# A hybrid decoder layer: X and Y products of the first two feed-forward blocks issued ahead of the column sums, T1 product third, activations loaded into their operand tiles

## The chip, the cores and the metric

The kernel runs on one core of one Trainium2 chip. The metric is the device time of one execution in microseconds (us); lower is better. The kernel before took 2458.94 us, the median of three runs (2458.13 to 2459.27).

## The reference

One inference step of one decoder layer in float32, for a prompt of 2048 tokens and for 8 decode tokens that each extend a cache of their own. The model width is 1024, the feed-forward width 2816. Cut to what matters:

```python
z = rms_norm(x, norm_mix_g) @ w_in              # q, k, v and the conv branch
...                                             # banded attention; GLU, conv of width 31, LayerNorm, silu
h = x + jnp.concatenate([attn_o, conv_o], axis=-1) @ w_out
fg, fu = jnp.split(rms_norm(h, norm_ffn_g) @ w_ffn_in, 2, axis=-1)
ffn_ext = jnp.concatenate([ffn_hist.astype(fg.dtype), fg], axis=1)
fc = causal_dwconv(ffn_ext, ffn_conv_w, ffn_conv_b)           # width 3
h = h + (jax.nn.gelu(fc, approximate=False) * fu) @ w_ffn_out
gate = jax.nn.sigmoid(rms_norm(h, norm_ple_g) @ w_ple_gate)
h = h + (p @ w_ple_proj) * gate
```

## The kernel before, in words

**Halves.** Tokens lie along the free dimension. The prompt is worked in two halves of 1024 tokens; half 1 also holds the 8 decode tokens. For each half come, in this order, the output projection (`w_out_unit`), the feed-forward up-projection with its gate (`ffn_in`, 22 blocks f of 128 gate rows and 128 up rows), and the down-projection (`ffn_out`). Half 0 does all three, then half 1. Last comes the gate with the per-layer embedding, in eight units m.

**Products.** TensorE (PE) multiplies float32 numbers as a high and a low part: `hilo` (L211) copies a tile into its high part on ScalarE (ACT, L212) and subtracts to get the low part on VectorE (DVE, L213), and every product takes three matmuls, hi·hi, hi·lo, lo·hi (L195, L196, L197).

**Seven products for eight.** `ffn_in` doesn't multiply the normed activations B by the weights directly. The activations of a half are cut in four blocks: features 0–511 and 512–1023 by tokens 0–511 and the rest, named B11, B21, B12, B22. The weights of an f are cut in four too, and seven block products of sums take the place of eight (a Strassen-Winograd scheme). Its operands are B11, B21, B22 and the sums T1 = B12 − B11, T2 = B22 − T1, T3 = B22 − B12 and T4 = B21 − T2. Every operand is split into high and low. On the weight side an f has four tiles: hg (the two blocks a11, a12), hs and ht (sums of blocks), and w (a22).

**The order of the products in an f.** X = hg·B11 (copied by ACT, L1152), Y = hg·B21 (summed by DVE into the gate rows, L1155), T2 added to X (copied, L1157), Z = ht·T1 (copied, L1160), T3 added to X (copied, L1162), B22 added to Z (summed by DVE, L1164), T4 added to X. X is one accumulator in PSUM; each copy has to be made before the next product may add to it. In half 0 a block is 512 columns wide, so an f has 84 matmuls of 512; in half 1 there are two blocks, of 256 and 264 columns (GROUPS), so 168 narrower ones. Then `gate` (L1131) makes gelu of the width-3 convolution: ACT L1133, DVE L1135 and L1136, for the decode tokens L1139 and L1140, and the gelu on ACT, L1141. DVE multiplies by the up rows (L1169) and the result is stored to DRAM (actd, L1170). The same is done for the second token block (L1172 to L1174).

**Weights.** Class W (L79 to L166) loads raw tiles of 512 KB (two buffers) through SyncE's queue (SP, L106), builds the sums on DVE (L138 to L141, all in place in the raw tiles but L138's s1f) and splits them into `whl` tiles (three buffers) and w (one buffer). For an f two raw tiles come: one with a11 and a12 (g), one with a21 and a22 (u). L138 adds a21 and a22; the raw tile of u is free when the low part of w is made.

**Building the operands.** `build_T` (L1070) waits for the row norms of the second token block: `stats` (L721) sums the columns of squares with matmuls by ones (L725), DVE copies the sums (L732), POOL takes the root, `bcast` (L735) transposes the result back to all partitions (rb, L738, L739), and a chain of some fifty DVE instructions (L1098 to L1117, with `hilo`'s) forms T2, T1, T3, B22 and T4. B11 and B21 are ready before, from the output projection's last part (`w_out_second`, `hn_k`).

**The down-projection.** `ffn_out` (L1182) loads the activations of a block from DRAM into a staging tile `as` (three buffers, L1193) and splits them with `hilo` into a tile `act`, which takes the place of an operand tile that is no longer needed.

**Beside it.** The width-31 convolution of half 1 runs on DVE (L403, L406) in pieces: `bg(ns)` issues as many of its steps as ns nanoseconds hold, after each f of the up-projection (5500) and each weight tile of the down-projection (3000).

**What sets the order.** A scheduler decides in which order the instructions stand on each engine, from the order of the code and from priorities. Each engine then works through its list in order; an instruction that waits holds back all behind it on its engine.

Of the kernel before, what the change touches and what calls it, by code (L numbers as in the profile page):

```python
# [7 lines left out]
F32 = mybir.dt.float32  # L8
# [9 lines left out]
KD = 8  # L18
# [15 lines left out]
def hybrid_layer_kernel(ctx: ExitStack, tc: tile.TileContext, I, O):  # L34
# [176 lines left out]
    def hilo(hi, lo, src):  # L211
        AC.copy(hi, src)  # L212
        DV.tensor_tensor(lo, src, hi.bitcast(F32), op=ALU.subtract)  # L213

    def rstd(dst, ss, tmp, cols, n):
# [529 lines left out]

    def hn_k(R, half, k, gi, rb, o, n):

        t = h_stage(half, k, o, n)
        lo = o % 512
        DV.scalar_tensor_tensor(t, t, gains[:, gi, k:k + 1], rb[:, o:o + n], op0=ALU.mult, op1=ALU.mult)  # L750
        hilo(R[k][:, 0, lo:lo + n], R[k][:, 1, lo:lo + n], t)
# [295 lines left out]
    def w_out_second(half, R, acc, rt, Rb, step, xs=None, xpool=None):  # L1047

        rb = st_tile("rb")
        for m in range(KD):  # L1050
            w_out_unit(half, R, m, C1[half], acc, xs, xpool)
            step()
            if m == 0:
                stats(acc, rt, 0, 512)
            if m == 1:
                bcast(rt, rb, 0, 512)
            for k in spread(m, 2):
                hn_k(Rb, half, k, 1, rb, 0, 512)
# [10 lines left out]

    def build_T(half, Rb, rb, acc, rt, w2, w1, wt, w3, wb, w4_):  # L1070
# [5 lines left out]
        t1 = [conv_p.tile([128, RW], F32, tag="co", bufs=5, name="t1f")[:, :n] for _ in range(4)]  # L1076
# [20 lines left out]
        for k in range(4):
            DV.scalar_tensor_tensor(b22[k], b22[k], gains[:, 1, k + 4:k + 5], bc, op0=ALU.mult, op1=ALU.mult)  # L1098
# [19 lines left out]
        return Rb[:4], Rb[4:], T2, T1, T3, B22, T4  # L1118

    def ffn_in(half, RT, f):  # L1120
        B11, B21, T2, T1, T3, B22, T4 = RT
        hg, (hs, ht), h22 = W.get(0), W.get(1), W.get(2)
        ext, sa, sb = st_tile("ext"), st_tile("snA"), st_tile("snB")
        if half == 0:
# [20 lines left out]
        last = GROUPS[half][-1][0]  # L1145
        for o, n in GROUPS[half]:
            n0 = min(n, 512 - o)
            s1, s2 = sa[:, o:o + n], sa[:, RW + o:RW + o + n]
            s5, s3 = sb[:, o:o + n], sb[:, RW + o:RW + o + n]
            X = mtile("X")  # L1150
# [11 lines left out]
            AC.copy(s3, X[:, :n])  # L1162
# [8 lines left out]
            GP.tensor_tensor(s3, s3, s5, op=ALU.add)  # L1171
        t = gate(512, tot)  # L1172
        DV.tensor_tensor(t[:, :tot], t[:, :tot], sb[:, RW:RW + tot], op=ALU.mult)
        SY.dma_start(actd[f][:, 512:512 + tot], t[:, :tot])  # L1174
        if half == 0:
            GP.tensor_copy(fhist[:, f, :], ext[:, HALF:HALF + 2])
        else:
            GP.tensor_copy(fnew[:, f, :], ext[:, HALF:HALF + 10])
        W.done(3)
        bg(5500)  # L1180

    def ffn_out(half, acc, where, step=None, done=None):  # L1182
# [4 lines left out]
        def prep(n):  # L1187
            while len(acts) < min(n, NF * len(pcs)):
                p, f = divmod(len(acts), NF)
                o, c = pcs[p]  # L1190
                a, = new_R("act", [where[len(acts)]])
                t = s2_tile("as")
                SY.dma_start(t[:, :c], actd[f][:, o:o + c])  # L1193
# [29 lines left out]


    RT = build_T(0, Rb, rb, acc, rts[0], [2] * 4, [2] * 4, [2] * 4, [1] * 4, [1] * 4, [2] * 4)
    step_ns[0] = 2500
    bg_list += [conv_piece(conv_p, 2), conv_piece(conv_p, 3), conv_dec(conv_p, st_p)]
    for f in range(NF):
        ffn_in(0, RT, f)
    acc2 = acc_tile("acc2")  # L1230
# [35 lines left out]
    Rb = new_R("bB", [1] * 4 + [2] * 4)  # L1266
    rb = w_out_second(1, Rm1, accB, rts[2], Rb, lambda: None, xs, co_tile)
    RT = build_T(1, Rb, rb, accB, rts[2], [2] * 4, [1] * 4, [1] * 4, [2] * 4, [1] * 4, [1] * 4)
    for f in range(NF):
        ffn_in(1, RT, f)  # L1270
    acc3 = acc_tile("acc3")
# [198 lines left out]
```

## Time and profile before

| | |
|---|---|
| Time, median of 3 runs | 2458.94 us (2458.13 to 2459.27) |
| The profiled execution's own time | 2448.64 us |
| Its span | 2446.8 us |
| Mean granted clock of TensorE | 0.985 |
| TensorE (PE) busy | 2343.6 us, 96% |
| VectorE (DVE) busy | 1743.2 us, 71% |
| ScalarE (ACT) busy | 1190.9 us, 49% |
| GpSimd (POOL) busy | 289.7 us, 12% |

The profile is of one execution. A row of its timeline has the start, the duration, the engine, the line of the kernel, the operation, and the output and inputs by the program's names with their shape; in brackets stands how long the engine was idle before it and what ended that. SPq is SyncE's queue of transfers. A row of the waits names an engine's line, what it waited for, and then the microseconds in total, the number of times and the longest. A row of the windows has a stretch of the span, its length, the busy time of PE, of PE's weight loads (PEld), DVE, ACT and POOL with their counts, PE's clock, the busy share of the transfer engines and GB/s.

### The profile page before, as it was taken

The page shows a single profiled execution, that of the slowest core. Times are in us where ns is not written, and L with a number is a line of the kernel's source. Part 1 is how long each engine was busy: PE and PEld are TensorE (multiplying, and loading weights), DVE is VectorE, ACT ScalarE, POOL GpSimd, SP SyncE. Part 2 cuts the span into 40 slices and gives each one's busy share as a digit, 9 for nine tenths or more (in the row PEclk, how much of TensorE's full clock was granted, in tenths as well). Part 3 has the DMA queues.
Part 4 walks back from the last instruction along what each step waited for, and adds up shares of the span by engine and source line. Part 5 has one row for each costly group of instructions (what it writes and reads, how often), then busy time and mean ns, then how long its engine had stood idle before and what let it go on. Part 6 is the DMA issues. An engine that isn't in the chain of part 4 may idle for free.

```text
span 2446.8 us, 36723 instructions
## 1 busy us (share of the span) xinstructions
PE 2343.6 (96%) x13691; PEld 2035.5 (83%) x13691; DVE 1743.2 (71%) x2943; ACT 1190.9 (49%) x2183; POOL 289.7 (12%) x354
## 2 busy tenths in 40 slices
PE   7899999999799999999999999999999899999999
PEld 6777778877587777878878888999999899988888
DVE  4999899766899999997634478666666554565553
ACT  4566676755444445444523445444444443444443
POOL 3312122100012111220001101111111000000000
PEclk9999999999899999999999999999999999999999
DMA  8543422367232222246745741222222565776664
GB/s 293 171 127 119 157 77 86 115 202 239 72 98 90 82 82 86 91 132 204 240 134 186 222 150 57 78 79 79 79 79 79 162 222 191 216 222 192 200 187 114
DMA packets 357076, 348.19 MB, mean 142 GB/s; under 512 B 24414, under 2 KB 277784, under 8 KB 352770
## 3 DMA queue, kind: packets, MB, share of 16 engines
q1 hardware_dynamic: 336610, 333.25, 43.4%
q10 hardware_dynamic: 20288, 12.60, 1.8%
q8 instruction: 107, 1.75, 0.3%
q14 instruction: 71, 0.58, 0.1%
HBM read 271.61 MB, written 75.78 MB: 142 GB/s over the span
## 4 chain that ended last, share of the span: by engine, by line
PE 62%; DVE 19%; DMA 10%; ACT 4%; issue 3%; POOL 1%; SPq 0%; ACTq 0%; DVEq 0%; POOLq 0%
DVE co L406 6%; PE fo L196 5%; PE fo L197 5%; PE fo L195 5%; PE X L195 4%; PE X L196 4%; PE X L197 4%; DVE whl L213 3%; DMA raw<-in_w_ffn_in 2%; PE pg L197 2%; PE pg L195 2%; PE pg L196 2%; PE wo L195 2%; PE wo L197 2%; PE wo L196 2%
## 5 line engine op out<-in xcount | busy, mean ns | idle before, releaser
L213 DVE TENSOR_TENSOR whl<-raw,whl 128x1024 fp32r<-128x1024 f32 (+1 forms) x314 | 360.2, 1147 | 242.4 <-ACT whl L212 241.6
L212 ACT CAST whl<-raw 128x1024 fp32r<-128x1024 f32 (+1 forms) x314 | 310.3, 988 | 274.5 <-PE fo L197 113.7
L406 DVE SCALAR_TENSOR_TENSOR co<-gi,cvec,co 128x512 f32<-128x512 f32 x480 | 372.0, 795 | 3.1
L195 PE MATMUL fo<-act,whl 128*128 128x512 f32 (+2 forms) x880 | 308.6, 352 | 11.3 <-ACT act L212 9.8
L196 PE MATMUL fo<-act,whl 128*128 128x512 f32 (+2 forms) x880 | 310.3, 353 | 0.1
L197 PE MATMUL fo<-act,whl 128*128 128x512 f32 (+2 forms) x880 | 309.4, 352 | 0.9 <-DVE whl L213 0.9
L195 PE MATMUL X<-T,whl 128*128 128x512 f32 (+2 forms) x528 | 172.2, 327 | 19.6 <-ACT T L212 11.8
L195 PEld LDWEIGHTS fo<-act,whl 128*128 128x128 f32 x880 | 166.1, 189 | 28.1 <-ACT act L212 10.7
L197 PEld LDWEIGHTS fo<-act,whl 128*128 128x128 f32 x880 | 166.4, 189 | 17.1 <-DVE whl L213 1.3
L196 PEld LDWEIGHTS fo<-act,whl 128*128 128x128 f32 x880 | 166.7, 189 | 16.3 <-DVE act L213 1.0
L196 PE MATMUL X<-T,whl 128*128 128x512 f32 (+2 forms) x528 | 171.7, 325 | 1.5 <-DVE T L213 1.5
L197 PE MATMUL X<-T,whl 128*128 128x512 f32 (+2 forms) x528 | 170.3, 323 | 0.0
L1171 POOL TENSOR_TENSOR snB<-snB 128x256 f32<-128x256 f32 (+1 forms) x66 | 89.9, 1363 | 542.4 <-ACT snB L1162 542.4
L1141 ACT ACTIVATE ft<-ft 128x512 f32<-128x512 f32 (+2 forms) x110 | 60.3, 548 | 162.5 <-DVE ft L1136 119.5
L195 PEld LDWEIGHTS X<-T,whl 128*128 128x128 f32 x528 | 100.5, 191 | 33.6 <-ACT T L212 14.5
L195 PE MATMUL ag<-r,whl 128*128 128x512 f32 (+2 forms) x320 | 115.8, 363 | 0.0
L196 PE MATMUL ag<-r,whl 128*128 128x512 f32 (+2 forms) x320 | 114.3, 358 | 0.0
L197 PE MATMUL ag<-r,whl 128*128 128x512 f32 (+2 forms) x320 | 113.2, 354 | 0.0
L196 PEld LDWEIGHTS X<-T,whl 128*128 128x128 f32 x528 | 100.4, 190 | 10.6 <-DVE T L213 3.2
L197 PEld LDWEIGHTS X<-T,whl 128*128 128x128 f32 x528 | 100.8, 191 | 8.3 <-DVE whl L213 0.4
L1133 ACT ACTIVATE ft<-ext,fvec 128x512 f32<-128x512 f32 (+2 forms) x110 | 80.1, 728 | 49.0 <-DVE ext L1164 24.8
L212 ACT CAST act<-as 128x512 fp32r<-128x512 f32 (+2 forms) x110 | 57.5, 537 | 77.6 <-DMA as<-actd 76.1
(376 smaller groups left out, 6399.9 us busy)
## 6 DMA issues: line engine op xcount, KB each, us to landing
raw<-in_w_ffn_out SPq DMA_DIRECT2D x110, 512.0 KB
raw<-in_w_ffn_in SPq DMA_DIRECT2D x88, 512.0 KB
whl<-agd SPq DMA_DIRECT2D x24, 1024.0 KB
hs<-h SPq DMA_DIRECT2D x80, 256.0 KB
raw<-in_w_out SPq DMA_DIRECT2D x32, 512.0 KB
raw<-in_w_ple_gate SPq DMA_DIRECT2D x32, 512.0 KB
actd<-ft SPq DMA_DIRECT2D x44, 256.0 KB
as<-actd SPq DMA_DIRECT2D x44, 256.0 KB
```

What stands on the lines that cost most here:

```text
L195: PE.matmul(ps, wh, xh, start=first, stop=False, skip_group_check=more)
L196: PE.matmul(ps, wh, xl, start=False, stop=False, skip_group_check=more)
L197: PE.matmul(ps, wl, xh, start=False, stop=last, skip_group_check=more)
L212: AC.copy(hi, src)
L213: DV.tensor_tensor(lo, src, hi.bitcast(F32), op=ALU.subtract)
L406: DV.scalar_tensor_tensor(co[c], t[:, i:i + QT], cvec[:, c, i:i + 1], co[c], op0=ALU.mult, op1=ALU.add)
L1133: AC.activation(t[:, :n], ext[:, 2 + o:2 + o + n], func=AF.Identity, scale=w2, bias=bi)
L1141: AC.activation(t[:, :n], t[:, :n], func=AF.Gelu)
L1171: GP.tensor_tensor(s3, s3, s5, op=ALU.add)
```

## The change

It does these things:

- `ffn_in` is cut in three functions. `first` does X and Y of a block, `second` the other five products and the gate of the first token block, `finish` the second gate. `ffn_in_all` issues `first` of f = 0 and f = 1 for all blocks ahead of `build_T` (and so ahead of the column sums), then `second` and `finish` of both, and from f = 2 on all three in turn.
- In `second` T1 comes third, before T2; the order is X, Y, T1, T2, T3, B22, T4.
- `build_T` makes T1 first, then T2. `w_out_second` keeps the unsplit B11 in four tiles (b11), so that T1 is one subtraction, where the kernel before subtracted the high part and then the low part (L1100, L1101).
- `ffn_out` loads the activations straight into the low half of the tile `act`; `hl_inplace` makes the high part and then the low part in place. The staging tile is gone.
- `bg` after an f goes from 5500 to 4300 in half 0 and to 0 in half 1, in the down-projection from 3000 to 3700.
- In the last stage the column sums of the third norm are taken after unit m = 3 and not after m = 0. The residual rows of the output projection in half 1 come from another pool, and a memset goes ahead.

```diff
+    def hl_inplace(t, n):
+
+        v = t[:, 1, :n].bitcast(F32)
+        hilo(t[:, 0, :n], t[:, 1, :n], v)
...
         for k in range(4):
+            DV.scalar_tensor_tensor(b12[k], b12[k], gains[:, 1, k:k + 1], bc, op0=ALU.mult, op1=ALU.mult)
+            tt(t1[k], b12[k], t1[k], op=ALU.subtract)
+            split(T1[k], t1[k])
+        for k in range(4):
             DV.scalar_tensor_tensor(b22[k], b22[k], gains[:, 1, k + 4:k + 5], bc, op0=ALU.mult, op1=ALU.mult)
-            DV.scalar_tensor_tensor(b12[k], b12[k], gains[:, 1, k:k + 1], bc, op0=ALU.mult, op1=ALU.mult)
-            tt(t1[k], b12[k], f32(Rb[k], 0), op=ALU.subtract)
-            tt(t1[k], t1[k], f32(Rb[k], 1), op=ALU.subtract)
             tt(t2[k], b22[k], t1[k], op=ALU.subtract)
             split(T2[k], t2[k])
-        for k in range(4):
-            split(T1[k], t1[k])
...
-            mm_prod(X[:, :n], hs, 0, T2, o, n, False)
-            AC.copy(s2, X[:, :n])
+            return X
+
+        def second(o, n, X, RT):
...
             Z = mtile("Z")
             mm_prod(Z[:, :n], ht, 512, T1, o, n, True)
             AC.copy(s5, Z[:, :n])
+            mm_prod(X[:, :n], hs, 0, T2, o, n, False)
+            AC.copy(s2, X[:, :n])
             mm_prod(X[:, :n], ht, 0, T3, o, n, False)
...
+    def ffn_in_all(half, Rb, build, ns, start=None):
+        gs = GROUPS[half]
+        u0 = ffn_in(half, Rb, 0)
+        x0 = [u0.first(*g) for g in gs]
+        W.topup(4)
+        u1 = ffn_in(half, Rb, 1, 3)
+        x1 = [u1.first(*g) for g in gs]
+        RT = build()
...
-                t = s2_tile("as")
-                SY.dma_start(t[:, :c], actd[f][:, o:o + c])
-                hilo(a[:, 0, :c], a[:, 1, :c], t[:, :c])
+                SY.dma_start(a[:, 1, :c].bitcast(F32), actd[f][:, o:o + c])
+                hl_inplace(a, c)
...
-        if m == 0:
+        if m == 3:
             stats(acc3, rts[3], 0, HALF + NDEC)
```

How the change moves instructions is shown at three places. In the changed file some lines have other numbers: L732 is L737, L1098 to L1100 are L1109 and L1110, L1133, L1135, L1136 and L1141 are L1148, L1150, L1151 and L1156, L1152 is L1167, L1155 is L1170, L1160, L1157 and L1162 are L1183, L1185 and L1187, L1164 is L1189, L1169 is L1194, L1173 is L1201.

On DVE at the build of half 0, before; accA holds the sums of squares, rt the column sums, s1f and raw are weights, tB is the start of the chain:

```order
L787 TENSOR_TENSOR accA<-accA,sqh 128x512
L732 COPY rt_5549<-st 128x4
L138 TENSOR_TENSOR s1f<-raw 128x512
L139 TENSOR_TENSOR raw<-raw 128x512
L1155 TENSOR_TENSOR ext<-Y,snA 128x512
L213 TENSOR_TENSOR whl<-raw,whl 128x1024
L1098 SCALAR_TENSOR_TENSOR tB<-tB,gains,rb 128x512
```

And in the changed kernel:

```order
L793 TENSOR_TENSOR accA<-accA,sqh 128x512
L138 TENSOR_TENSOR s1f<-raw 128x512
L139 TENSOR_TENSOR raw<-raw 128x512
L1170 TENSOR_TENSOR ext<-Y,snA 128x512
L737 COPY rt_5549<-st 128x4
L213 TENSOR_TENSOR whl<-raw,whl 128x1024
L140 TENSOR_TENSOR raw<-s1f,raw 128x512
L141 TENSOR_TENSOR raw<-raw 128x512
L1170 TENSOR_TENSOR ext<-Y,snA 128x512
L213 TENSOR_TENSOR whl<-raw,whl 128x1024
L1109 SCALAR_TENSOR_TENSOR tB<-tB,gains,rb 128x512 x2
```

The copy of the column sums has moved behind L138, L139 and the first sum of Y, and more weight work and the sum of Y of f = 1 stand ahead of the chain. On PE the column sums stand behind all 24 matmuls of X and Y of f = 0, where eleven of X stood ahead of them before; three of the broadcast's four transposes follow soon, and the fourth stands behind 20 matmuls of X and Y of f = 1. In half 1 the column sums stand behind the 48 matmuls of X and Y of f = 0.

On DVE in a steady f of half 1, before; ft is the gate's tile, ext its rows:

```order
L1173 TENSOR_TENSOR ft<-ft,snB 128x520
L1135 SCALAR_TENSOR_TENSOR ft<-ext,fvec,ft 128x256
L138 TENSOR_TENSOR s1f<-raw 128x512
L1136 SCALAR_TENSOR_TENSOR ft<-ext,fvec,ft 128x256
L139 TENSOR_TENSOR raw<-raw 128x512
L1164 TENSOR_TENSOR ext<-Z,snA 128x256
```

And in the changed kernel, in 18 of the 22 f's:

```order
L1201 TENSOR_TENSOR ft<-ft,snB 128x520
L138 TENSOR_TENSOR s1f<-raw 128x512
L1150 SCALAR_TENSOR_TENSOR ft<-ext,fvec,ft 128x256
L139 TENSOR_TENSOR raw<-raw 128x512
L1151 SCALAR_TENSOR_TENSOR ft<-ext,fvec,ft 128x256
L1189 TENSOR_TENSOR ext<-Z,snA 128x256
```

The two weight instructions have moved one place ahead each, past one instruction of the gate. On PE the 12 matmuls of T3 stand behind 4 of the 12 of B22 in half 1 (behind 4, 5 or 6 in half 0), and the other 8 behind T3.

On ACT in the last block of half 1, in the changed kernel (before, all copies of act stood behind the gelu of the last gate); snA and snB are the copies of X and Z, act the activations of the down-projection:

```order
L1167 COPY snA<-X 128x264
L212 CAST act<-act 128x384
L212 CAST whl<-raw 128x1024
L1148 ACTIVATE ft<-ext,fvec 128x256
L1183 COPY snB<-Z 128x264
L212 CAST act<-act 128x384 x3
L1185 COPY snA<-X 128x264
L212 CAST act<-act 128x384
L1156 ACTIVATE ft<-ft 128x256
L212 CAST act<-act 128x384 x3
L1187 COPY snB<-X 128x264
```

Eight copies of loaded activations now stand ahead of the copy L1187, four of them ahead of L1185. On SP the loads of these activations stand ahead of the stores of the last f.

More of the change, by code (lines that the diff above doesn't have):

```diff
@@ L744, in h_stage, with hn_k @@
         return t[:, :n]
-    def hn_k(R, half, k, gi, rb, o, n):
-        t = h_stage(half, k, o, n)
+    def hn_k(R, half, k, gi, rb, o, n, keep=None):
+        src = h_stage(half, k, o, n)
+        t = src if keep is None else keep
         lo = o % 512
-        DV.scalar_tensor_tensor(t, t, gains[:, gi, k:k + 1], rb[:, o:o + n], op0=ALU.mult, op1=ALU.mult)
+        DV.scalar_tensor_tensor(t, src, gains[:, gi, k:k + 1], rb[:, o:o + n], op0=ALU.mult, op1=ALU.mult)
         hilo(R[k][:, 0, lo:lo + n], R[k][:, 1, lo:lo + n], t)
@@ L1049, in w_out_second @@
         rb = st_tile("rb")
+        b11 = []
+        if half:
+            for k in range(KD):
+                GP.memset(Rb[k][:, :, 512:512 + NDEC].bitcast(F32), 0.0)
         for m in range(KD):
@@ L1057, in w_out_second @@
             for k in spread(m, 2):
-                hn_k(Rb, half, k, 1, rb, 0, 512)
-        return rb
+                if k < 4:
+                    b11.append(conv_p.tile([128, RW], F32, tag="co", bufs=5, name="b11"))
+                    if half:
+                        GP.memset(b11[k][:, 512:], 0.0)
+                hn_k(Rb, half, k, 1, rb, 0, 512, b11[k][:, :512] if k < 4 else None)
+        return rb, b11
     Rb = new_R("bA", [1] * 8)
-    rb = w_out_second(0, Rm1, acc, rts[0], Rb, dec_step)
+    rb, b11 = w_out_second(0, Rm1, acc, rts[0], Rb, dec_step)
     for _ in range(20):
@@ L1066, in hybrid_layer_kernel, with build_T @@
     RP[2] = ctx.enter_context(tc.tile_pool(name="R2", bufs=1, side="right", reuse_waits="tile"))
-    def build_T(half, Rb, rb, acc, rt, w2, w1, wt, w3, wb, w4_):
+    def build_T(half, Rb, rb, b11, acc, rt, w2, w1, wt, w3, wb, w4_):
         n = 512 + (NDEC if half else 0)
@@ L1075, in build_T @@
         b22, b12 = [t[:, 0, :n] for t in tmp], [t[:, 1, :n] for t in tmp]
-        t1 = [conv_p.tile([128, RW], F32, tag="co", bufs=5, name="t1f")[:, :n] for _ in range(4)]
+        t1 = [t[:, :n] for t in b11]
         t2 = [conv_p.tile([128, RW], F32, tag="gi", bufs=2, name="t2f")[:, :n] for _ in range(2)]
@@ L1117, in build_T, with ffn_in @@
             split(T4[k], t2[k])
[L1118 to L1123, printed above, removed]
+        return T2, T1, T3, B22, T4
+    class FfnIn:
+        pass
+    def ffn_in(half, Rb, f, base=0):
+        B11, B21 = Rb[:4], Rb[4:]
+        hg = W.get(base)
+        ext, sa = st_tile("ext"), st_tile("snA")
+        sbs = []
         if half == 0:
@@ L1145, in ffn_in, with first @@
         last = GROUPS[half][-1][0]
-        for o, n in GROUPS[half]:
+        def first(o, n):
             n0 = min(n, 512 - o)
-            s1, s2 = sa[:, o:o + n], sa[:, RW + o:RW + o + n]
-            s5, s3 = sb[:, o:o + n], sb[:, RW + o:RW + o + n]
+            s1 = sa[:, o:o + n]
             X = mtile("X")
@@ L1155, in ffn_in @@
             DV.tensor_tensor(ext[:, 2 + o:2 + o + n0], Y[:, :n0], s1[:, :n0], op=ALU.add)
-            mm_prod(X[:, :n], hs, 0, T2, o, n, False)
-            AC.copy(s2, X[:, :n])
+            return X
+        def second(o, n, X, RT):
+            T2, T1, T3, B22, T4 = RT
+            (hs, ht), h22 = W.get(1), W.get(2)
+            if not sbs:
+                sbs.append(st_tile("snB"))
+            sb = sbs[0]
+            n0 = min(n, 512 - o)
+            s2, s5, s3 = sa[:, RW + o:RW + o + n], sb[:, o:o + n], sb[:, RW + o:RW + o + n]
             Z = mtile("Z")
@@ L1171, in ffn_in, with finish @@
             GP.tensor_tensor(s3, s3, s5, op=ALU.add)
[L1172 to L1180, printed above, removed]
+        def finish(ns):
+            sb = sbs[0]
+            t = gate(512, tot)
+            DV.tensor_tensor(t[:, :tot], t[:, :tot], sb[:, RW:RW + tot], op=ALU.mult)
+            SY.dma_start(actd[f][:, 512:512 + tot], t[:, :tot])
+            if half == 0:
+                GP.tensor_copy(fhist[:, f, :], ext[:, HALF:HALF + 2])
+            else:
+                GP.tensor_copy(fnew[:, f, :], ext[:, HALF:HALF + 10])
+            W.done(3)
+            bg(ns)
+        u = FfnIn()
+        u.first, u.second, u.finish = first, second, finish
+        return u
+    def ffn_in_all(half, Rb, build, ns, start=None):
[6 more added lines that the diff above has]
+        RT = build()
+        if start:
+            start()
+        for u, xs in ((u0, x0), (u1, x1)):
+            for g, X in zip(gs, xs):
+                u.second(*g, X, RT)
+            u.finish(ns)
+        for f in range(2, NF):
+            u = ffn_in(half, Rb, f)
+            for g in gs:
+                u.second(*g, u.first(*g), RT)
+            u.finish(ns)
     def ffn_out(half, acc, where, step=None, done=None):
@@ L1222, in ffn_out, with start_conv @@
                 done(p)
[L1225 to L1229, printed above, removed]
+    def start_conv():
+        step_ns[0] = 2500
+        bg_list.extend([conv_piece(conv_p, 2), conv_piece(conv_p, 3), conv_dec(conv_p, st_p)])
+    ffn_in_all(0, Rb, lambda: build_T(0, Rb, rb, b11, acc, rts[0], [2] * 4, [2] * 4, [2] * 4, [1] * 4, [1] * 4, [2] * 4),
+               4300, start_conv)
     acc2 = acc_tile("acc2")
@@ L1266, in hybrid_layer_kernel @@
     Rb = new_R("bB", [1] * 4 + [2] * 4)
[L1267 to L1270, printed above, removed]
+    rb, b11 = w_out_second(1, Rm1, accB, rts[2], Rb, lambda: None, xs)
+    ffn_in_all(1, Rb, lambda: build_T(1, Rb, rb, b11, accB, rts[2], [2] * 4, [1] * 4, [1] * 4, [2] * 4, [1] * 4, [1] * 4), 0)
     acc3 = acc_tile("acc3")
```

5 lines of the change are left out of this document (1 added, 4 removed).

## The prediction

> **What bounds the kernel now.** I read the page first, then the table of the stages that the change touches, then PE's waits, then the timeline at each long wait. The page says that TensorE (PE) sets the time.
>
> ```profile
> span 2446.8 us, 36723 instructions
> PE 2343.6 (96%) x13691; PEld 2035.5 (83%) x13691; DVE 1743.2 (71%) x2943; ACT 1190.9 (49%) x2183; POOL 289.7 (12%) x354
> ```
>
> The change removes no matmul, so it can win only what PE idles or runs below full clock. The stages, in us: length, then busy time of PE, PEld, DVE, ACT and POOL, then PE's clock, DMA share and GB/s. 600–700 and 1420–1530 are the two builds of the operands, 700–1080 and 1530–1915 the up-projection of each half, 1915–1960 the start of the down-projection of half 1.
>
> ```profile
> 600.00:700.00 100.00, 84.04 (x362) 64.07 (x361) 87.28 (x136) 47.03 (x77) 7.09 (x11) 0.90 0.33 102
> 700.00:1080.00 380.00, 373.44 (x1607) 299.90 (x1606) 377.46 (x540) 173.16 (x261) 70.25 (x58) 1.00 0.29 89
> 1420.00:1530.00 110.00, 98.22 (x711) 92.81 (x712) 84.91 (x151) 51.50 (x102) 14.35 (x15) 0.91 0.28 89
> 1530.00:1915.00 385.00, 381.58 (x3159) 379.23 (x3158) 241.03 (x450) 181.99 (x359) 42.84 (x75) 1.00 0.27 80
> 1915.00:1960.00 45.00, 38.21 (x230) 37.67 (x229) 23.42 (x36) 20.67 (x35) 0.95 (x2) 0.92 0.60 186
> ```
>
> PE idles 16.0 and 11.8 us in the builds, 6.6 and 3.4 in the up-projections, 6.8 at that start. A matmul costs 373.44/1607 = 0.232 us in half 0 and 381.58/3159 = 0.121 in half 1; a vector (DVE) instruction about 87.28/136 = 0.64. Where the waits are:
>
> ```profile
> PE X L195 <- ACT T L212: 13.7, 6, 8.1
> PE fo L195 <- ACT act L212: 9.8, 2, 6.8
> PE st L725 <- DVE acc L787: 5.3, 3, 3.2
> PE X L195 <- ACT snA L1152: 4.4, 5, 2.1
> ```
>
> A part of the change touches each of the four: 33.2 us in all.
>
> **The change part by part.**
>
> *Building the operands, half 0.* On DVE the row sums (L732), the first (L1098) and the last instruction of the chain, L138 (it waits for a weight transfer), and PE's waits:
>
> ```profile
> 624.62 0.16 DVE L732 COPY rt<-st 128x4 f32<-128x4 f32 x1 [1.77 <-PE st L725]
> 626.73 0.69 DVE L138 TENSOR_TENSOR s1f<-raw 128x512 f32<-128x512 f32 x1 [1.95 <-DMA raw<-in_w_ffn_in]
> 626.22 0.65 PE L738 MATMUL rb<-ident,rt 128*128 128x128 f32 x4 [0.83 <-POOL rt L217]
> 631.44 0.75 DVE L1098 SCALAR_TENSOR_TENSOR tB<-tB,gains,rb 128x512 f32<-128x512 f32 x1
> 666.56 0.69 DVE L213 TENSOR_TENSOR T<-t2f,T 128x512 fp32r<-128x512 f32 x1
> 637.29 0.79 PE L195 MATMUL X<-T,whl 128*128 128x512 f32 x1 [8.10 <-ACT T L212]
> 669.82 0.50 PE L195 MATMUL X<-T,whl 128*128 128x512 f32 x1 [1.65 <-ACT whl L212]
> ```
>
> The chain takes 35.1 us of DVE, and PE can't finish before it. After the change the order puts L138, L139 and the sum of Y ahead of L732's copy (now L737): 626.73 + 3 × 0.64 = 628.7, 4.1 us later. Then come the products of f=1, of which 20 matmuls stand ahead of the last transpose of the broadcast: 628.7 + 1.6 (624.62 to the transposes at 626.22) + 20 × 0.232 = 634.9, then the sum of Y and a weight's low part, about 2.5: the chain starts near 637.5, 6 us later than 631.44. It is four instructions shorter (2.6 us), so it ends some 3 us later, while PE has done the X and Y of f=1 in between, 24 × 0.232 = 5.6 us. I take −3 (bounds −10, if all of the 8.10 and 1.65 goes, to +1).
>
> *Half 1* has the same shape with narrower blocks:
>
> ```profile
> 1454.00 0.76 DVE L1098 SCALAR_TENSOR_TENSOR tB<-tB,gains,rb 128x520 f32<-128x520 f32 x1 [3.51 <-ACT rb L739]
> 1458.70 0.58 PE L195 MATMUL Z<-T,whl 128*128 128x256 f32 x1 [3.15 <-ACT T L212]
> ```
>
> The order puts all 48 matmuls of f=0 before the sums, and more DVE work ahead of them; by the same walk the chain starts about 10 us later and, four instructions shorter, ends 7.5 later. By then the order has let PE do 76 more matmuls, 76 × 0.121 = 9.2 us. 7.5 − 9.2 = −1.7, and about +1 for matmuls below full clock behind the new idle: −1 (−6, if the 3.15 goes as well and the walk is 2 us too slow, to +3). Together −4 (−10 to +3, since both won't fall to one end).
>
> The Trainium skill ("TensorE: Matmul & The Clock Gate", Part 1 "The HAM clock gate (the "warmup" mystery)") says that the clock halves after about 3.4 us idle and is back after as much sustained work. The clocks 0.90 and 0.91 in the two build rows agree that long idles cost more than themselves; by the page, new stalls of about 1 us, such as those below, cost their length alone.
>
> *Activations loaded in place.*
>
> ```profile
> 1925.51 0.38 SPq L1193 DMA_DIRECT2D as<-actd  x1
> 1930.06 0.51 ACT L212 CAST act<-as 128x384 fp32r<-128x384 f32 x1 [2.89 <-DMA as<-actd]
> 1930.62 0.69 PE L195 MATMUL fo<-act,whl 128*128 128x384 f32 x1 [6.79 <-ACT act L212]
> 1087.95 1.60 PE L195 MATMUL fo<-act,whl 128*128 128x512 f32 x4 [3.03 <-ACT act L212]
> ```
>
> With no staging tile the first loads go ahead of the last store, during the last f, so 6.79 + 3.03 = 9.8 us and the slow matmuls behind (clock 0.92 over the 45 us of the last stage row, 3.6 us) can go: up to −14 with both halves. But ScalarE (ACT) runs in order, and four of its copies of act, each waiting for its transfer (1925.51 to 1930.06: 4.55 us from issue to copy), now stand ahead of L1185 and eight ahead of L1187, and PE waits for both: I charge 2 us a half, under half a transfer, since the first can go when X of the last block is done, three products (3 × 12 × 0.121 = 4.4) before L1185 is due. Net −10 (−14 to −2).
>
> *Row sums of the last norm after unit 3.*
>
> ```profile
> 2198.86 1.14 PE L725 MATMUL st<-ones,acc 128*128 128x1 f32 x6 [3.25 <-DVE acc L787]
> ```
>
> That wait lies ahead of one unit's matmuls; three units later acc is long done: −3.2.
>
> *Up-projection, half 0.* DVE is busy 377.46 of 380 us there, PE idles 6.6. Conv work goes from ten to about eight instructions per f, T1 now covers the L1152 copy (PE's fourth wait), and T3 has four or five B22 matmuls before it, 5 × 0.232 = 1.16, for a path that takes 0.75 at 264 columns (below) and more at 512: just enough. I take −6, most of the idle time (bounds −6.6 and +6, as a late copy could stall each f by 0.5).
>
> *Up-projection, half 1: the loss.* One f, from T4's last matmul to the next T4; the middle rows are DVE and ACT in engine order:
>
> ```profile
> 1655.61 0.29 PE L197 MATMUL X<-T,w 128*128 128x264 f32 x1
> 1657.07 0.68 DVE L213 TENSOR_TENSOR w<-raw,w 128x512 fp32r<-128x512 f32 x1
> 1661.13 0.48 DVE L1135 SCALAR_TENSOR_TENSOR ft<-ext,fvec,ft 128x256 f32<-128x256 f32 x1
> 1662.25 0.69 DVE L138 TENSOR_TENSOR s1f<-raw 128x512 f32<-128x512 f32 x1 [0.64 <-DMA raw<-in_w_ffn_in]
> 1662.86 0.48 DVE L1136 SCALAR_TENSOR_TENSOR ft<-ext,fvec,ft 128x256 f32<-128x256 f32 x1
> 1663.25 0.68 DVE L139 TENSOR_TENSOR raw<-raw 128x512 f32<-128x512 f32 x1
> 1663.37 0.42 ACT L1141 ACTIVATE ft<-ft 128x256 f32<-128x256 f32 x1 [1.39 <-DVE ft L1136]
> 1663.69 0.35 ACT L1162 COPY snB<-X 128x256 f32<-128x256 f32 x1
> 1664.24 0.29 PE L195 MATMUL X<-T,w 128*128 128x256 f32 x1
> 1519.91 0.69 DVE L138 TENSOR_TENSOR s1f<-raw 128x512 f32<-128x512 f32 x1 [1.40 <-DMA raw<-in_w_ffn_in]
> 1705.92 0.39 PE L195 MATMUL X<-T,w 128*128 128x256 f32 x1 [1.24 <-ACT snB L1162]
> 1889.07 0.69 DVE L138 TENSOR_TENSOR s1f<-raw 128x512 f32<-128x512 f32 x1 [0.73 <-DMA raw<-in_w_ffn_in]
> ```
>
> The weights close a loop: w's low part frees the raw tile, the next transfer lands 5.2 us after it, L138 waits for it, L1136 stands behind L138, the gelu behind L1136, the copy L1162 behind the gelu on ACT, and T4 needs that copy. T4 starts 1.99 us after L138, with nothing to spare: where L138 comes later, PE stalls (1.24 at 1705.92). Between the first and last L138 quoted lie 18 f's, 369.16/18 = 20.51 us each, against 168 × 0.121 = 20.3.
>
> In 18 of the 22 f's the order after is L138, L1135, L139, L1136 (now L138, L1150, L139, L1151). L1135, which now lies in the shadow of the transfer, and L139 come between L138 and the gelu: 0.39 + 0.60 = 1.0 us (spacings 1662.86 to 1663.25 and 0.64 at most). As the loop is closed over T4, each f grows by it: 18 × 1.0 = +18. Further, T3 now follows T2 with only four B22 matmuls between, 5 × 0.121 = 0.60 from T2's last start, against the copy's path:
>
> ```profile
> 1612.05 0.28 PE L197 MATMUL X<-T,whl 128*128 128x264 f32 x1
> 1612.37 0.38 ACT L1162 COPY snB<-X 128x264 f32<-128x264 f32 x1 [0.22 <-PE X L197]
> ```
>
> 0.32 + 0.38 + 0.05 = 0.75, so 0.15 short. In the first block the T4 wait absorbs it; in the second 20 × 0.15 = 3, of which I keep 1, since w's low part waits for DVE, not for T4. Half 1: +19 (+10, if half the f's hide it, to +28, with each transfer 0.4 us later).
>
> The Trainium skill ("DMA: Bandwidth & Descriptors", "Anatomy of one DMA — SWDGE (gpsimd) path") fits a transfer as 2.0 us plus bytes/436e3, an estimate of 3.2 us for these 512 KB. The rows have 5.2 from w's low part to L138. By the page's figure the loop would have over a us to spare, and the sum would be about 20 lower; the rows decide, and I give it the chance of the second rival.
>
> *Conv moved into the down-projection, residual rows from another pool:* the first is under PE, the second early: +1.5 (0 to +6).
>
> Sum: −4 − 10 − 3.2 − 6 + 19 + 1.5 = −2.7 us. The profiled execution took 2448.64 (span 2446.8), so about 2446 there; the median of the runs, 2458.94, lies 10 above it, and I carry the difference over: **2456**.
>
> **The rivals.**
> 1. *A slower kernel through half 0.* If the raw transfer there lands later than DVE reaches L138, the same order (L138 before the gate, gelu before L1185 on ACT) stalls T3 in every f. For it: DVE had only 2.5 us of idle time in half 0, so the trace doesn't show when transfers land. Against: w's low part comes sooner with less conv ahead. It decides from about 0.3 us of lateness; 20 f's × 0.7 = +14 in place of −6 makes the sum +17: 2476, or 2466 if half the f's do it.
> 2. *The wait of L138 goes* (transfers spread otherwise, landing 1 us sooner): half 1 pays only the 3 of T3 and loses the 20 × 0.2 it has now: −1 in place of +19: 2436. Against: of the nineteen L138's between the two quoted, all waited for the transfer, 19.8 us together:
>
> ```profile
>   DMA raw<-in_w_ffn_in: 19.8, 19
> ```
>
> 3. *The builds fill as the code is written*: PE runs X and Y of two f's through the whole wait, 8.10 + 3.15 + 1.65 and the half clock: −14 in place of −4: 2446.
> 4. *The loads in place give nothing*, since ACT's in-order waits for transfers only move the stall into the last f: 0 in place of −10: 2466.
>
> **How the numbers follow.** Changes under 0.2%, 4.9 us, count as the same: that is what a measurement of this kernel can tell. Forecast, no change, 0.43 (2451 to 2462, faster 0.07 of it, slower 0.06); rival 1, 0.18; rival 2, 0.09; rival 3, 0.22; rival 4, 0.08. Faster: 0.07 + 0.09 + 0.22 = 0.38; slower: 0.06 + 0.18 + 0.08 = 0.32; same 0.30. The range goes to rival 3 and below it to where half of rival 2 is in, and up to rival 1's half and its upper bounds: 2441 to 2472.
>
> **What would show it.** Right: the period between T4's of half 1 is near 21.5 us, with waits of T4 on the copy L1187 of about 1 us in 18 f's; waits of T3 on L1185 of 0.15; no wait of fo on act over 2 us; no wait of st on acc at the end. Wrong: a period of 20.5 or less in half 1 (the loop), a longer one than 20.2 in half 0 (rival 1), PE idling under 15 us in the two builds together (rival 3).

## The result, and the profile after

The changed kernel is slower: 2479.35 us median of four runs (2474.0 to 2484.41) beside 2458.53 for the kernel before (2455.77 to 2459.27), a ratio of 1.0086 with a 95% interval of 1.006 to 1.0113. The forecast was 2456, no change, in a range of 2441 to 2472. The profiled execution of the changed kernel took 2484.41 us. Its page:

```profile
span 2482.6 us, 36658 instructions
PE 2365.6 (95%) x13691; PEld 2044.1 (82%) x13691; DVE 1733.6 (70%) x2935; ACT 1187.8 (48%) x2185; POOL 291.4 (12%) x358
```

PE's matmuls are the same in number and it is busy for longer: some ran at a lower clock, and a short gap counts as busy, since a row of half 1 lasts 0.28 us where the next matmul starts 0.12 after it. DVE and ACT have no more work than before. Some of PE's longest waits in the whole program, in the touched stages:

```profile
PE X L195 <- ACT snB L1187: 22.1, 19, 2.7
PE Z L195 <- ACT T L212: 7.8, 2, 4.9
PE xres L778 <- DMA xr<-in_x_prompt: 6.0, 6, 1.9
PE X L195 <- ACT snA L1185: 5.4, 7, 2.3
PE st L730 <- DVE acc L793: 0.7, 1, 0.7
```

The waits of fo on act (9.8 us before) are gone, and so is the one of the last sums on acc (3.2 before); the 0.7 on acc lies in the output projection of half 1. In their place T4 waits 22.1 us in all for the copy L1187, which in the kernel before was L1162:

```profile
PE X L195 <- ACT snB L1162: 3.6, 4, 1.4
```

The stages, first build, up-projection of half 0, second build, up-projection of half 1 and the start of the second down-projection (this program runs some 5 to 40 us later than before, so the stretches are set anew):

```profile
600.00:700.00 100.00, 87.53 (x361) 65.00 (x362) 80.67 (x131) 47.61 (x80) 13.85 (x10) 0.91 0.36 107
700.00:1085.00 385.00, 378.54 (x1619) 300.93 (x1618) 356.19 (x508) 181.56 (x271) 55.08 (x58) 1.00 0.30 93
1458.00:1530.00 72.00, 58.38 (x383) 53.77 (x382) 54.65 (x96) 33.44 (x64) 15.61 (x13) 0.83 0.17 53
1530.00:1965.00 435.00, 413.06 (x3305) 401.72 (x3305) 252.65 (x473) 186.60 (x378) 54.70 (x77) 1.00 0.25 77
1960.00:2000.00 40.00, 39.25 (x249) 39.02 (x248) 29.10 (x48) 24.89 (x45) 1.22 (x2) 1.00 0.84 272
```

PE idles 22 us in the up-projection of half 1 (3.4 before) and under one at the start of the down-projection (6.8 before). One f of half 1, with the rows that the prediction showed of the kernel before:

```profile
1592.93 0.28 PE L197 MATMUL X<-T,w 128*128 128x264 f32 x1
1594.55 0.69 DVE L213 TENSOR_TENSOR w<-raw,w 128x512 fp32r<-128x512 f32 x1
1595.26 0.59 SPq L106 DMA_DIRECT2D raw<-in_w_ffn_in  x1
1600.25 0.69 DVE L138 TENSOR_TENSOR s1f<-raw 128x512 f32<-128x512 f32 x1 [1.55 <-DMA raw<-in_w_ffn_in]
1600.86 0.48 DVE L1150 SCALAR_TENSOR_TENSOR ft<-ext,fvec,ft 128x256 f32<-128x256 f32 x1
1601.26 0.69 DVE L139 TENSOR_TENSOR raw<-raw 128x512 f32<-128x512 f32 x1
1601.86 0.48 DVE L1151 SCALAR_TENSOR_TENSOR ft<-ext,fvec,ft 128x256 f32<-128x256 f32 x1
1602.38 0.42 ACT L1156 ACTIVATE ft<-ft 128x256 f32<-128x256 f32 x1 [3.06 <-DVE ft L1151]
1602.70 0.35 ACT L1187 COPY snB<-X 128x256 f32<-128x256 f32 x1
1603.10 0.39 PE L195 MATMUL X<-T,w 128*128 128x256 f32 x1 [1.11 <-ACT snB L1187]
1603.33 0.28 PE L196 MATMUL X<-T,w 128*128 128x256 f32 x1
```

T4 starts 2.85 us after L138, in eighteen f's. In the kernel before it started 1.85 or 1.86 after it in fourteen of nineteen f's and later in the others; the 1.99 of the prediction's f, read as having nothing to spare, had 0.14 to spare. The chain that the prediction drew is there link by link. T3's short wait is too small for the waits, and is seen in the starts alone; 0.12 is the spacing of two matmuls that wait for nothing:

```profile
1599.10 0.28 PE L195 MATMUL Z<-B,whl 128*128 128x256 f32 x1
1599.37 0.38 PE L195 MATMUL X<-T,whl 128*128 128x256 f32 x1
1599.59 0.28 PE L196 MATMUL X<-T,whl 128*128 128x256 f32 x1
```

To compare the programs stage by stage, the trace of each was cut at the same matmuls: the first X of a half, the last T4 of f = 1 and of f = 21, the first and the last fo of a half. In us; "before" and "changed" have two profiles each (the second are before_again and changed_again, below):

| stage | before | changed | difference of the means | forecast |
|---|---|---|---|---|
| build and f = 0, 1, half 0 | 63.0, 62.9 | 61.6, 60.5 | −1.9 | −3 |
| f = 2 to 21, half 0 | 400.6, 399.9 | 403.6, 402.9 | +3.0 | −6 |
| to the first fo, both halves | 11.4, 11.3 | 0.4, 0.4 | −11.0 | −10 |
| down-projection, half 0 | 254.4, 254.3 | 256.8, 256.2 | +2.2 | +1.5 with the next |
| output projection, half 1 | 104.2, 104.3 | 110.2, 110.1 | +5.9 | |
| build and f = 0, 1, half 1 | 66.0, 66.0 | 69.2, 67.6 | +2.4 | −1 |
| f = 2 to 21, half 1 | 410.2, 407.5 | 443.0, 442.7 | +34.0 | +19 |
| down-projection, half 1 | 254.6, 255.8 | 254.5, 252.0 | −2.0 | 0 |
| last stage | 258.0, 256.6 | 253.6, 253.6 | −3.7 | −3.2 |

The sum is +29, where the runs differ by 21. Ahead of these stages two profiles of one program, the kernel before, differ by 7.5 (621.0 and 628.5 us to the first X), so the stages of two profiles are to be compared, not their ends.

### The profile page after: what moved, and what is told of

Read it like the earlier page. It is cut to its first block, busy times and chain, and to the rows that moved or that the text cites. A ratio compares the mean times of both kernels' runs of the same rounds, so it can differ in the third digit from the quotient of the medians.

```text
span 2482.6 us, 36658 instructions
## 1 busy us (share of the span) xinstructions
PE 2365.6 (95%) x13691; PEld 2044.1 (82%) x13691; DVE 1733.6 (70%) x2935; ACT 1187.8 (48%) x2185; POOL 291.4 (12%) x358
## 5 line engine op out<-in xcount | busy, mean ns | idle before, releaser
L411 DVE SCALAR_TENSOR_TENSOR co<-gi,cvec,co 128x512 f32<-128x512 f32 x480 | 366.9, 788 | 3.0
L1196 POOL TENSOR_TENSOR snB<-snB 128x256 f32<-128x256 f32 (+1 forms) x66 | 83.9, 1272 | 609.7 <-ACT snB L1187 603.7
L1156 ACT ACTIVATE ft<-ft 128x512 f32<-128x512 f32 (+2 forms) x110 | 60.1, 548 | 165.6 <-DVE ft L1151 123.3
L195 PE MATMUL X<-T,w 128*128 128x512 f32 (+2 forms) x264 | 86.7, 330 | 25.4 <-ACT snB L1187 22.1
L1148 ACT ACTIVATE ft<-ext,fvec 128x512 f32<-128x512 f32 (+2 forms) x110 | 80.5, 732 | 45.5 <-DVE ext L1189 25.8
```

The costliest lines, as they stand in the source:

```text
L195: PE.matmul(ps, wh, xh, start=first, stop=False, skip_group_check=more)
L411: DV.scalar_tensor_tensor(co[c], t[:, i:i + QT], cvec[:, c, i:i + 1], co[c], op0=ALU.mult, op1=ALU.add)
L1148: AC.activation(t[:, :n], ext[:, 2 + o:2 + o + n], func=AF.Identity, scale=w2, bias=bi)
L1156: AC.activation(t[:, :n], t[:, :n], func=AF.Gelu)
```

## The experiments

The **theory** was that of the prediction, with its size mended: a loop runs from T4 through w's low part, the freed raw tile, its next transfer, L138, the gate, the gelu and the copy L1187 to the next T4, and two more DVE instructions in it make each f longer; T3's short cover adds its waits. The **rivals** were that T1's third place alone is the loss, that the order on DVE costs PE time by itself, and that the weights come too late whoever waits for them.

**gate_first.** In half 1 the first weight sum is queued behind the gate on DVE:

```diff
+                    with tc.issue_after(W.behind):      # L1151 of this f's first block
                         DV.tensor_tensor(t, a21, a22, op=ALU.add)
```

> The changed kernel, with one edit in half 1: the weight sum L138 stands behind the gate's second instruction (L1151) on DVE, in every f; the product order stays X, Y, T1, T2, T3, B22, T4. Loop theory: T4 no longer waits for the transfer that L138 waits for, since nothing between L138 and the copy L1187 is left; the period of half 1 falls from 22.1 to about 20.7 us (20.1 of matmuls and 0.5 for T3's two short waits), 1.4 us times 20: some 2451 in place of 2479. Product-order rival (T1 third leaves T3 too little cover, and that is the loss): the period stays over 21.6, the time over 2469. Transfer rival (the weights simply come too late in half 1, whoever waits for them): the period stays near 22, with the wait at another product; 2475 or more.

Measured: 2452.16 us beside 2450.2 of before on that chip, ratio 1.0004 (0.9988 to 1.0019), and a period of 20.73 us. The period is the theory's. The time falls less than the 28 us expected: by the ratios it is some 20 below the changed kernel, as the edge also makes the build with f = 0 and 1 longer (73.7 us for 69.2 and 67.6). The loss against before is gone with one edge on DVE, and T3's short cover, which stayed, is not the larger part of it.

**copy_first.** In half 1 the gelu of the first block is queued behind the copy L1187 on ACT:

```diff
-            AC.copy(s3, X[:, :n])
+            c3 = AC.copy(s3, X[:, :n])
...
+            with tc.issue_after(c3.ins):
                 AC.activation(t[:, :n], t[:, :n], func=AF.Gelu)
```

> The changed kernel, with one edit in half 1: in the first block ACT makes the copy L1187 ahead of the gelu L1156, DVE keeps L138, L1150, L139, L1151. Loop theory: the chain is cut at its ACT link in place of its DVE link, and the same 1.4 us an f go: period about 20.7, time about 2451, though L138 still waits for its transfer ahead of the gate. A theory that DVE's order itself costs PE time (rival): no gain, 2475 or more. Product-order rival: period over 21.6, time over 2469.

Measured: 2448.26 us, ratio 0.999 (0.9973 to 1.0008), period 20.73. In the trace of this kernel DVE waits for the same transfer, in the same order, and T4 no longer cares:

```profile
1595.72 0.69 DVE L138 TENSOR_TENSOR s1f<-raw 128x512 f32<-128x512 f32 x1 [1.63 <-DMA raw<-in_w_ffn_in]
1596.33 0.48 DVE L1150 SCALAR_TENSOR_TENSOR ft<-ext,fvec,ft 128x256 f32<-128x256 f32 x1
1596.48 0.37 ACT L1188 COPY snB<-X 128x256 f32<-128x256 f32 x1 [1.77 <-PE X L197]
1597.22 0.28 PE L195 MATMUL X<-T,w 128*128 128x256 f32 x1
1598.32 0.42 ACT L1157 ACTIVATE ft<-ft 128x256 f32<-128x256 f32 x1 [1.47 <-DVE ft L1151]
```

All waits for the transfer in that stage, of this kernel and of the changed one:

```profile
  DMA raw<-in_w_ffn_in: 31.0, 19
```

```profile
  DMA raw<-in_w_ffn_in: 32.5, 19
```

DVE waits as long in the one as in the other, but the copy (here L1188) comes 1.84 us ahead of the gelu. The order on DVE is no loss in itself, and the transfers aren't late for PE: both rivals fall. The same period by two different cuts means that what is left over the 20.15 of the best kernels, 0.58 an f, is T3's two waits.

**t1_fourth.** The product order of before, X, Y, T2, T1, T3, B22, T4, in both halves of the changed kernel:

```diff
+            mm_prod(X[:, :n], hs, 0, T2, o, n, False)
+            AC.copy(s2, X[:, :n])
             Z = mtile("Z")
             mm_prod(Z[:, :n], ht, 512, T1, o, n, True)
             AC.copy(s5, Z[:, :n])
-            mm_prod(X[:, :n], hs, 0, T2, o, n, False)
-            AC.copy(s2, X[:, :n])
```

> The changed kernel with the product order of before in both halves (T1 between T2 and T3); DVE in half 1 then has L1150, L138, L1151, L139, as in the kernel before. Loop theory: the chain from L138 to T4 is 1.85 us again, the period of half 1 20.5, 1.6 us times 20 less: 2447; in half 0 the waits of T2 on the copy of X come back, +3 to +8, so 2450 to 2455. Product-order rival: the same for half 1; what tells the two apart is gate_first. If half 0 gains as well, T1 third was a loss there too.

Measured: 2436.13 us, ratio 0.9947 (0.9925 to 0.997); period of half 1 20.30; half 0's twenty f's 397.4 us. Here the expectation for half 0 failed, to the good: it gains 6 against the changed kernel and 3 against before. So T1 third was a loss there too. In half 1 DVE has L1150, L138, L1151, L139 again in 18 f's, the order of the kernel before. So it was T1's third place that let the scheduler move L138 ahead: the loop's loss and T3's waits both come from it. PE's waits in half 0's up-projection show it, first those of the changed kernel, then those of this one:

```profile
PE X L195 <- ACT snA L1185: 4.7, 6, 2.3
PE Z L195 <- ACT snB L1183: 0.8, 2, 0.6
```

```profile
PE X L195 <- ACT snA L1167: 1.7, 3, 1.0
PE X L195 <- ACT snB L1187: 1.1, 1, 1.1
```

The new waits of T3 on L1185 come to more than what is left of T2's on L1167 once T1 is fourth again: 1.7 us, where the kernel before had 4.4 on the same copy (L1152). That it is the lighter conv load that makes the copy earlier is likely, and was not tried alone.

**all_three.** The two cuts of the loop and T1 fourth, in half 1 alone.

> The changed kernel, in half 1 with the gate ahead of L138, the copy L1187 ahead of the gelu, and T1 fourth; half 0 as changed. Loop theory: nothing of the loop is left ahead of T4 and T3 has a whole product of cover, so the period is near the 20.1 of its matmuls, 2.0 us times 20 less than the changed kernel: about 2439, faster than both kernels. Transfer rival: the period stays at 21 or more, since the weights come no sooner; 2459 or more. If it lies at 2447, the gate and copy order is worth nothing beside the product order.

Measured: 2441.14 us, ratio 0.9961 (0.9945 to 0.9978); period 20.17, as expected. It is faster than before and no faster than t1_fourth: half 0 keeps T1 third (401.4 us), and the edge that holds L138 back costs the first f's: build and f = 0, 1 of half 1 take 73.8 us, in gate_first 73.7, in t1_fourth 67.3.

**before_sums_first.** The kernel before, with the gate code of half 1's first block moved behind the weights' code, so that DVE has the order of the changed kernel, and ACT the copy ahead of the gelu:

```diff
+                b1, b2 = tc.issue_after(W.sums[0]), tc.issue_after(W.sums[1])   # L138, L139
...
+            todo.append((o, n0, X, s3, s5))
+            for o, n0, X, s3, s5 in todo if o == last else ():
-            t = gate(o, n0)
+                t = gate(o, n0)
```

> The kernel before, in half 1 with the gates of both token blocks issued behind the weights' sums, so that DVE has L138, L1135, L139, L1136 as in the changed kernel, while ACT makes the copy L1162 ahead of the gelu. Loop theory: DVE's order costs nothing once the copy that T4 waits for no longer stands behind the gelu; the period of half 1 falls from 20.5 to 20.2 us, 0.3 times 20 = 6 less than before. DVE-order rival (the order on DVE is the loss by itself): the period rises by 1, 20 us more than before.

Measured: the period is 20.14 us, every f between 20.13 and 20.15, as the theory has it and against the DVE-order rival. The time, 2452.21 us beside 2449.22, ratio 1.0007 (0.9995 to 1.0018), doesn't show the 6 us. By the stages the up-projection of half 1 gives 5 to 7, the build ahead of it takes 2.3 back (68.3), and the rest lies in the 1 us by which other stages differ between profiles; which of them is real was not settled.

**before_direct_load.** The kernel before, with the activations loaded in place:

```diff
-                t = s2_tile("as")
-                SY.dma_start(t[:, :c], actd[f][:, o:o + c])
-                hilo(a[:, 0, :c], a[:, 1, :c], t[:, :c])
+                v = a[:, 1, :c].bitcast(F32)
+                SY.dma_start(v, actd[f][:, o:o + c])
+                hilo(a[:, 0, :c], a[:, 1, :c], v)
```

> The kernel before with the activations of the down-projection loaded straight into the operand tile, and nothing else. Forecast's term: 10 less than before (6.79 and 3.03 of waits and the slow matmuls behind go, some 4 come back through ACT's in-order waits for transfers). Rival: ACT's waits only move the stall into the last f of each half, within 3 of before.

Measured: 2430.52 us beside 2449.22, ratio 0.9925 (0.9904 to 0.9947): 18.7 less, nearly twice the forecast. In its trace the time to the first fo falls from 11.3 to 0.4 us and the down-projections are 2.7 and 2 to 3 shorter. ACT's waits for the transfers take a part back: in the last f of half 0 T4 waits 2.3 for L1162 and the matmuls behind run at a clock of 0.50 for 3.4 us, so that this f takes 23.64 us where the kernel before takes 19.49. These 16 us, less 5 more in half 0's up-projection, 4.2 of them in that f, are most of what its profile has (its execution, 2438.8, was the longest of four); where the runs find the rest stays open.

**best.** The changed kernel with T1 fourth in both halves, the copy ahead of the gelu in half 1, and the residual rows of half 1 in two tiles of their own:

```diff
+    def gi_tile():
+        return conv_p.tile([128, 30 + QT], F32, tag="gi", bufs=2, name="xrB")[:, :QT]
...
-    rb, b11 = w_out_second(1, Rm1, accB, rts[2], Rb, lambda: None, xs)
+    rb, b11 = w_out_second(1, Rm1, accB, rts[2], Rb, lambda: None, xs, gi_tile)
```

> The changed kernel with T1 fourth in both halves, in half 1 the copy L1187 ahead of the gelu, and the residual rows of half 1's output projection in a pool of their own with two buffers. Loop theory: half 1 at 20.2 a period, 2 less in all than t1_fourth, half 0 at 19.9; the stage of the output projection 5 less, as PE's waits for xr go: 2436 - 7 = 2429 on a chip where before takes 2450, a ratio near 0.991. If the xr waits come from the transfers and not from the pool, that stage stays at 110 and the ratio is 0.994.

Measured: 2427.04 us, ratio 0.9904 (0.9884 to 0.9923); period 20.16, half 0 398.1 us, the output projection of half 1 103.7 where the changed kernel takes 110. The expectation's other case, transfers that are late by themselves, falls. The waits for xr came from the pool: its `st` tiles also hold that stage's results, and a row can't be loaded before one is free.

**best_no_early.** The same, with the early products taken out:

```diff
-        u0 = ffn_in(half, Rb, 0)
-        x0 = [u0.first(*g) for g in gs]
-        W.topup(4)
-        u1 = ffn_in(half, Rb, 1, 3)
-        x1 = [u1.first(*g) for g in gs]
         RT = build()
...
-        for f in range(2, NF):
+        for f in range(NF):
```

> The kernel best without the early products: X and Y of f = 0 and f = 1 stand behind the building of the operands, as in the code of before. Forecast's term for the builds: 4 more than best. Rival 3 (the builds fill as the code is written): 14 more than best. No effect or a loss from the early products in half 1, where the build took 67 us with them and 66 without: within 2 of best.

Measured: 2423.92 us, ratio 0.9886 (0.9867 to 0.9905). The intervals overlap, so no loss is shown; a gain of 4 by the early products, or of 14, is ruled out. The builds take 60.3 and 66.2 us without them, 60.2 and 68.2 with them.

**changed_again.** The changed kernel itself, not edited.

> The changed kernel itself once more, on the chip and in the call of the others. If the loss is one of the program: a period of 22.1 us in half 1 and the ratio 1.0086 found first, within its interval 1.006 to 1.011. If it was one of that execution (transfers late by chance): a shorter period, a ratio near 1.

Measured: 2472.49 us beside 2452.6, ratio 1.0073 (1.0051 to 1.0096), period 22.13. The loss is the program's. Its profiled execution was again the longest of its four (2480.99; the others 2467.63 to 2473.36), which is why the stages sum to more than the runs differ by.

**before_again.** The kernel before itself, not edited.

> The kernel before itself, for a second profile. If the first profile was a typical one, the steady f's of half 1 take 20.5 us again and the stages ahead of half 0's up-projection 621; the profiles of the other kernels had 622 to 629 there, so I expect 625 and a span of 2446 to 2452.

Measured: 2452.62 us, span 2450.8, period 20.38, and 628.5 us ahead of half 0's up-projection.

**three_edits.** The kernel before with the load in place, the copy ahead of the gelu in half 1, and the last sums after unit 3 (the diffs are those above and the change's own).

> The kernel before with three edits alone: activations loaded straight into the operand tile, in half 1 the copy L1162 ahead of the gelu, and the column sums of the last norm after unit 3. By the runs so far: -18.7 of the direct load, -6 of the loop cut, -3 of the sums: 2449 - 28 = 2421, a ratio of 0.989, as good as best_no_early. If best_no_early's gain needs the new way to build the operands or T1's subtraction: 2428 or more.

Measured: 2428.88 us, ratio 0.9902 (0.9883 to 0.9921), period 20.16. Three edits of a few lines give what the mended change gives; by the intervals best, best_no_early and three_edits can't be told apart. The expected ratio, 0.989, lies in the interval; so does the other case, 2428 beside 2449, and the run doesn't decide between them.

## Why the prediction was wrong

**The failed step** is the term "Up-projection, half 1: the loss", put at +19. Its mechanism was right: gate_first and copy_first cut it at two places and brought the same period. Its size was not: +34 in the profiles. Two parts were mis-sized. The first is T3's cover. The prediction put 0.15 a block, let T4's wait absorb one of the two and kept 1 us of the 3. A wait that short costs PE 0.25 in all: 1599.10 to 1599.37 is 0.15 over the spacing of 0.12, as forecast, and the matmul behind it is 0.10 late as well. With the loop cut both blocks pay, 20.73 − 20.15 = 0.58 an f or 11.6 us; with the loop uncut the second block pays 0.25. The second part is the loop itself: to the 1.0 us of the two DVE instructions (2.85 for 1.85, as forecast) come 0.16 in w's low part (1.62 us after T4 for 1.46) and 0.2 to 0.4 from w's low part to L138 (5.8 us in the mean, for 5.6 and 5.35 in the two profiles of before). Cutting the loop gave 22.14 − 20.73 = 1.41 an f, 28 us, in the profiles, and 17 to 24 by the ratios of the runs.

**Up-projection of half 0, −6: wrong in sign.** The cover of 1.16 us was called just enough on the strength of a path of 0.75 at 264 columns. In the rows above T3 waited for L1185 six times. At the longest the copy stood on ACT behind the gelu, and the gelu waited for DVE, where weight work stood among the gate's instructions:

```profile
835.42 0.69 DVE L138 TENSOR_TENSOR s1f<-raw 128x512 f32<-128x512 f32 x1 [0.40 <-DMA raw<-in_w_ffn_in]
839.62 0.75 DVE L1151 SCALAR_TENSOR_TENSOR ft<-ext,fvec,ft 128x512 f32<-128x512 f32 x1
840.41 0.63 ACT L1156 ACTIVATE ft<-ft 128x512 f32<-128x512 f32 x1 [2.37 <-DVE ft L1151]
840.94 0.57 ACT L1185 COPY snA<-X 128x512 f32<-128x512 f32 x1
841.56 0.50 PE L195 MATMUL X<-T,whl 128*128 128x512 f32 x1 [2.27 <-ACT snA L1185]
```

Another, of 1.39 us, lies in the last f, behind copies of act that waited for their transfers. That f takes 22.4 and 21.8 us where the kernel before takes 19.49: 2.6 of the +3.0. The other nineteen f's together are 0.4 longer than before. t1_fourth takes 4.6 off these nineteen and 1.2 off the last, so T1's third place cost 6, and what else changed in the nineteen, most likely the lighter conv, was worth some 4. Rival 1 named the stage, the sign and the path, with the gelu ahead of L1185, but not this size: +3, not +14.

**The builds, −4: half 0 as forecast in sign, half 1 not.** By starts, the chain (L1109 after the first X) begins 20.5 us after in half 0 (10.5 before) and 24.3 after in half 1 (7.5 before), not 16.5 and 17.5 as walked. The early products fill the time but put it off by as much: best_no_early shows no gain from them. The sign in half 0 was luck: the stage takes 60.3 us without them and 60.2 with them, so the gain over the kernel before's 63 is not theirs. Rival 3 falls with that. What the walk left out in half 1 are PE's own waits among them:

```profile
1468.83 0.59 PE L195 MATMUL Y<-bB,whl 128*128 128x264 f32 x1 [2.24 <-DVE rt L733]
1472.68 0.69 PE L743 MATMUL rb<-ident,rt 128*128 128x128 f32 x2 [3.04 <-POOL rt L222]
1485.53 0.80 PE L195 MATMUL Z<-T,whl 128*128 128x256 f32 x2 [2.94 <-ACT T L212]
```

**The loads in place, −10, and the last sums, −3.2: near by the stages** (−11.0 and −3.7). But the −11.0 stands before what ACT's waits take back in the last f's, for which the prediction charged 2 us a half: in half 0 2.6 in the changed kernel, with T1's third place, and 4.2 in before_direct_load; in half 1 at most 1 in any kernel that loads in place. Alone and by the runs the loads gave 18.7. So rival 4 has its path but not its size: ACT's queue gave a part of the stall back and not all of it.

**Conv and residual rows, +1.5: too little,** +8 with the down-projection's +2.2. The prediction called the residual rows early; the 6 us came from a pool that had too few tiles, as best shows; 4.3 of them are listed as waits of PE for xr in that stage.

**Rival 2,** the transfers' landing sooner, falls: L138 waited 32.5 us in 19 f's for them. The estimate of 3.2 us that the prediction set beside them comes from a section on transfers that GpSimd issues, as its heading says. These go through SyncE's queue, and in the up-projection of half 1 they took 4.2 us or more from issue to L138 in the kernel before and 4.6 or more in the changed one.

So of the −2.7 that was forecast, the terms that were wins nearly held (−3.2, −10) or were lost to T1's third place, and the one large loss was drawn rightly and made too small. The bounds of that term, +10 to +28, didn't hold what the profiles have. The medians of the runs differ by 8 less than the stages sum to; if all of that lay here, the term would be 26. Nor is it the only miss: of the 32 us by which the stages exceed the forecast, 15 are this term's, 9 lie in half 0's up-projection, 7 in the conv and residual rows and 4 to 5 in the builds, and other stages give some 3 back. The range of the whole, which took the other terms at their middle, was too narrow on that side.

## What to carry to other kernels

When a trace shows an accumulator's next product starting at the same distance behind an unrelated instruction in f after f (1.85 or 1.86 us behind L138 in fourteen of nineteen), that instruction is in a closed loop with it, and an instruction that a new order puts between the two can be paid in full each time round, as the 1.0 us was here. Cut such a loop at the cheapest link, here by putting a 0.35 us copy ahead of a gelu on ACT, before moving anything else. And test the edits of a bundle one by one: three small ones made this kernel 1% faster, while the bundle that held two of them made it 0.9% slower.

## What the runs showed of the hardware that was not expected

A wait of PE costs more than the wait: after one, the next matmul also starts late, 0.22 us behind in place of 0.12 (1599.37 to 1599.59, 1603.10 to 1603.33), and this even for waits of 0.15 us.

Waits of 2 to 3 us can halve the clock. In the changed kernel's second build PE waited 2.24 and 3.04 us, as shown above, with less than 1 us of work between, and later 2.94; the stretches behind ran at half clock:

```profile
1466.00:1470.00 4.00, 1.39 (x7) 0.87 (x6) 2.95 (x6) 0.00 (x0) 1.08 (x1) 0.73 0.27 81
1470.00:1474.00 4.00, 1.32 (x6) 1.32 (x7) 1.41 (x3) 0.37 (x1) 2.37 (x4) 0.50 0.00 0
1486.00:1490.00 4.00, 3.36 (x15) 2.76 (x14) 4.00 (x8) 0.71 (x2) 0.00 (x0) 0.50 0.02 7
```

A clock of 0.73 over the first row means that it fell at about 1467.8, when the first wait had lasted some 1.3 us. A wait of 2.3 us can go either way. Behind the one of T3 in half 0, 2.27 us, the first profile of the changed kernel kept its clock (first row below) and that f took 22.47 us. Behind the same wait, 2.27 us, changed_again lost it (second row) and the f took 23.87. What decides was not found.

```profile
841.50:845.00 3.50, 3.44 (x15) 2.81 (x16) 3.50 (x7) 0.34 (x2) 0.00 (x0) 1.00 0.00 0
844.60:847.80 3.20, 3.20 (x9) 2.53 (x8) 3.20 (x6) 0.00 (x0) 0.00 (x0) 0.50 0.00 0
```

The Trainium skill ("TensorE: Matmul & The Clock Gate", Part 1 "The HAM clock gate (the "warmup" mystery)") puts the halving after about 3.4 us idle. By these rows less was enough, and the rows decide. That stalls of about 1 us leave the clock alone, the trace bears out: the up-projection of half 1 has seventeen of 0.77 to 1.66 us and ran at 1.00, as its row above shows, but for a stretch behind the one longer stall, of 2.71 us:

```profile
1870.70:1874.00 3.30, 3.30 (x17) 3.30 (x17) 0.42 (x1) 0.00 (x0) 0.00 (x0) 0.50 0.12 40
```
